# Output projections that accumulate in five PSUM banks in turn instead of two

## The chip, the cores and the metric

The kernel runs on one core of one Trainium2 chip. The metric is the device time of one execution in microseconds (us). Before the change it is 3158.45 us, the median of three runs that took 3152.99 to 3162.29 us.

## The reference

Four layers act in turn on x, 1024 tokens by 1024 features, all in float32. Every one of them ends in a projection back to 1024 features, and that last projection is what the change is about:

```python
# layer 1: dilated attention          return (o * jax.nn.silu(z)) @ w_out
# layer 2: state space (S5)           return (y * jax.nn.silu(z)) @ w_out
# both:                               x = x + rms_norm(h, post_norm)
# layers 3 and 4: hybrid layers (convolution, retention, neighbourhood attention)
y = jnp.concatenate([y_conv, y_ret, y_na], axis=-1) @ w_out
x_new = layer_norm(DEEPNORM_ALPHA * x + gate[:, None] * y, ln_g, ln_b)
```

The first hybrid layer (here: layer 0 of the hybrid part) also carries a context of 256 tokens through the same projection; the second (layer 1) does not.

## The kernel before

**Numbers in halves.** A float32 product is made of three products of two halves: every operand is split into a high part and a remainder (`aTh`/`aTl` for the activations, `wh`/`wl` or `wo` for the weights), and `mm3` (line 163) issues high·high, high·low and low·high for each of eight blocks k of 128 features. So one output tile of 128 tokens by 512 features is 24 matmuls of 128x128 by 128x512 that accumulate in one PSUM bank.

**PSUM.** The eight banks are dealt out by tag: `mm` has two (line 143, all projections), `T` two (transposes), `S` three (scores of the attentions, states of the retention), `O` one. A tile of a tag takes the bank of the tile that many places earlier under the same tag, and waits until the last reader of that one is done. An output tile's bank is read by VectorE (line 1166 after the first two layers, line 2074 in the hybrid layers), which multiplies by a gain or a gate; after the first two layers ScalarE also squares it (line 1165).

**The last projections.** `out_tile` (line 1102) makes one tile. `out_rms` (line 1144) calls it for eight blocks of 128 tokens and two halves of the features, 16 tiles, after dilated attention and after the state space layer; `out_ln` (line 2036) does so in the hybrid layers, 20 tiles in layer 0 (eight blocks and two of the context) and 16 in layer 1. Behind each block follow the norm and, but for the last layer, transposes of the result (line 219).

**What is late at the start of a hybrid layer's last projection.** The activations come in slabs of 256 tokens: each is fetched from DRAM by ScalarE's queue (lines 2013, 2014, into `ys`) and split by ScalarE and VectorE (lines 2017, 2018). Two output tiles come out of every block of 128 tokens, so a slab feeds four output tiles. The weight blocks 0 to 2 are split early into buffers of the attention that are free by then; blocks 3 to 5, and a slab that lies in the same pool, can start only when the neighbourhood attention has left its pool, after its last matmuls (`O`, lines 133 and 139, in the context 1944). The attention's end runs between the first output tiles on TensorE: transposes of the probabilities (lines 1861, 1870, 1932), products with the values, and a transpose for the weights of the sum (line 1903).

**Order.** The order of every engine's instructions is fixed when the kernel is built: a scheduler places them by its own estimates and by the waits that buffers and banks make. An engine then works strictly in that order.

Of the kernel before, what the change touches and what calls it, by code (L numbers as in the profile page):

```python
# [11 lines left out]
F32 = mybir.dt.float32  # L12
# [8 lines left out]
S = 1024  # L21
# [54 lines left out]
class Ker:  # L76
    def __init__(self, nc, tc, es, A):
        self.nc, self.tc, self.A = nc, tc, A
        self.cp = es.enter_context(tc.tile_pool(name="cp", bufs=1))
        self.big = es.enter_context(tc.tile_pool(name="big", bufs=1))  # L80
        self.ps = es.enter_context(tc.tile_pool(name="ps", bufs=1, space=PSUM))
        self.dr = es.enter_context(tc.tile_pool(name="dr", bufs=1, space=DRAM))
        self.wp = es.enter_context(tc.tile_pool(name="wp", bufs=1, reuse_waits="tile"))
        self.bg = deque()
        self.hot = deque()
        self.rate = 0.0
        self.acc = 0.0
        self.n = 0
        self.ident = self.cp.tile([128, 128], F32, name="ident")
        make_identity(nc, self.ident)  # L90
        self.mhalf = self.cp.tile([128, 1], F32, name="mhalf")
        nc.vector.memset(self.mhalf, -0.5)
        self.ones = self.cp.tile([128, 1], F32R, name="ones")
        nc.vector.memset(self.ones.bitcast(F32), 1.0)
        self.cact = self.cp.tile([128, 2, 8], F32, name="cact")
        self.hp = self.cp.tile([128, 1], F32, name="hp")
        nc.vector.memset(self.hp, math.pi / 2)
        self.fh = self.cp.tile([128, 32], F32R, name="fh")
        self.rest = self.cp.tile([128, 32], F32, name="rest")
        self.aTh = self.big.tile([128, 8, 1024], F32R, name="aTh")  # L100
        self.aTl = self.big.tile([128, 8, 1024], F32R, name="aTl")

    def uid(self, s):
        self.n += 1
        return f"{s}_{self.n}"
# [995 lines left out]

    def out_tile(self, i, nh, ks, aT=None):

        ps = self.mm()
        aT = (self.aTh, self.aTl) if aT is None else aT
        tt, c = slice(i * 128, i * 128 + 128), slice(nh * 512, nh * 512 + 512)
        self.mm3(ps, [((aT[0][:, k, tt], aT[1][:, k, tt]), (self.wo[k][0][:, c], self.wo[k][1][:, c]))
                      for k in ks])
        return ps
# [1065 lines left out]
```

## Time and profile before

| | |
|---|---|
| median of three runs | 3158.45 us (3152.99 to 3162.29) |
| profiled execution | 3156.31 us, its span 3154.1 us |
| TensorE (PE) busy | 3060.2 us, 97% of the span |
| VectorE (DVE) busy | 1894.4 us, 60% |
| ScalarE (ACT) busy | 1189.4 us, 38% |
| GpSimd (POOL) busy | 588.6 us, 19% |
| granted clock of TensorE, mean | 0.989 of full |

TensorE works nearly all the time. What it doesn't work, or works at half its clock, has to be looked for in short stretches; the table only says that such stretches are few.

### The profile page before, as it was taken

To read this page: it belongs to the slowest core of one execution; us is meant where nothing else is said; L and a number is where in the kernel's file an instruction comes from. 1 tells how busy PE (TensorE), PEld (TensorE's weight loads), DVE (VectorE), ACT (ScalarE), POOL (GpSimd) and SP (SyncE) were. 2 spreads that over 40 slices of the span, in tenths; PEclk is the share of its full clock that TensorE was granted. 3 is DMA by queue.
4 is the path that set the end of the run, shared out by engine and by line. 5 is a ranking of instruction groups with operands and counts; after the bars stand their busy time and mean duration, and the time that the engine had idled before them with its cause. 6 is when DMAs were issued, how large, how long until landed. Compare 5 with 4: busy or idle time off the path is not lost. (4 is left out here: it accounts for less than half of the span.)

```text
span 3154.1 us, 47830 instructions
## 1 busy us (share of the span) xinstructions
PE 3060.2 (97%) x18100; PEld 2539.2 (81%) x18100; DVE 1894.4 (60%) x4099; ACT 1189.4 (38%) x2492; POOL 588.6 (19%) x762
## 2 busy tenths in 40 slices
PE   8999999999999999999999999999998999999998
PEld 6777878778887878787878888788887888888877
DVE  4676676677766647665654634455566754455564
ACT  4222555455555554322431112244352212234351
POOL 0365120221211201110003122310001112220001
PEclk9999999999999999999999999999999999999999
DMA  5455232332333235565342211122125321121132
GB/s 200 152 187 175 69 102 83 88 103 83 96 95 97 76 102 181 184 181 156 121 144 90 81 43 57 48 82 60 48 72 170 104 73 56 54 81 52 51 119 94
DMA packets 332603, 324.11 MB, mean 103 GB/s; under 512 B 30073, under 2 KB 273492, under 8 KB 332372
## 3 DMA queue, kind: packets, MB, share of 16 engines
q1 hardware_dynamic: 324020, 312.79, 32.4%
q10 hardware_dynamic: 8352, 8.26, 0.8%
q8 instruction: 143, 2.34, 0.3%
q14 instruction: 88, 0.72, 0.1%
HBM read 248.29 MB, written 72.69 MB: 102 GB/s over the span
## 5 line engine op out<-in xcount | busy, mean ns | idle before, releaser
L172 PE MATMUL mm<-aTh,wh 128*128 128x512 f32 x2304 | 916.9, 398 | 12.9 <-DVE qk L427 2.9
L172 PE MATMUL mm<-aTl,wh 128*128 128x512 f32 x2304 | 913.0, 396 | 0.4 <-DVE aTl L225 0.2
L172 PE MATMUL mm<-aTh,wl 128*128 128x512 f32 x2304 | 912.8, 396 | 0.5 <-DVE wl L159 0.4
L172 PEld LDWEIGHTS mm<-aTh,wh 128*128 128x128 f32 x2304 | 436.6, 190 | 103.5 <-issue 4.6
L172 PEld LDWEIGHTS mm<-aTh,wl 128*128 128x128 f32 x2304 | 435.9, 189 | 87.0 <-DVE wl L159 1.4
L172 PEld LDWEIGHTS mm<-aTl,wh 128*128 128x128 f32 x2304 | 436.3, 189 | 84.5 <-issue 1.0
L159 DVE TENSOR_TENSOR wl<-wr,wh 128x1024 fp32r<-128x1024 f32 x156 | 197.6, 1267 | 221.9 <-ACT wh L158 220.6
L158 ACT ACTIVATE wh<-wr 128x1024 fp32r<-128x1024 f32 x156 | 164.9, 1057 | 325.3 <-PE mm L172 266.9
L172 PE MATMUL mm<-wo,aTh 128*128 128x512 f32 x768 | 247.3, 403 | 17.4 <-DVE ys L2074 9.0
L479 ACT ACTIVATE sb<-sb,st 128x128 f32<-128x128 f32 (+1 forms) x384 | 170.2, 445 | 240.0 <-DVE st L477 235.1
L1217 DVE SCALAR_TENSOR_TENSOR ma<-mw,cact,ma 128x256 f32<-128x256 f32 x336 | 184.3, 553 | 15.3 <-DMA mw<-in_w_mod 8.6
L172 PEld LDWEIGHTS mm<-wo,aTh 128*128 128x128 f32 x768 | 146.1, 193 | 51.3 <-DVE ys L2074 8.2
L477 DVE CUSTOM_DVE_ANT_0 sb<-S,bt 128x128 f32<-128x128 f32 (+1 forms) x384 | 125.5, 344 | 52.1 <-PE T L490 37.0
L172 PE MATMUL mm<-wo,aTl 128*128 128x512 f32 x384 | 153.0, 398 | 0.0
L431 POOL CAST qk<-kz 64x512 fp32r<-64x512 f32 x64 | 64.8, 1012 | 323.1 <-ACT kz L425 311.6
L1831 ACT ACTIVATE nsb<-nsb,nmn 128x640 f32<-128x640 f32 (+1 forms) x108 | 85.6, 793 | 101.8 <-DVE nmn L1828 97.7
L172 PE MATMUL mm<-vh,aTl 128*128 128x512 f32 x288 | 113.8, 395 | 0.0
L172 PE MATMUL mm<-vl,aTh 128*128 128x512 f32 x288 | 113.6, 394 | 0.0
L172 PE MATMUL mm<-vh,aTh 128*128 128x512 f32 x288 | 113.5, 394 | 0.0
L490 PE MATMUL T<-ident,sb 128*128 128x128 f32 x560 | 102.3, 285 | 9.9 <-ACT PT L493 6.1
L172 PE MATMUL mm<-cTh,wh 128*128 128x256 f32 x352 | 101.6, 289 | 0.6 <-DVE nk L1515 0.6
L172 PE MATMUL mm<-cTh,wl 128*128 128x256 f32 x352 | 100.3, 285 | 0.6 <-DVE wl L159 0.6
(449 smaller groups left out, 5624.3 us busy)
## 6 DMA issues: line engine op xcount, KB each, us to landing
wr<-in_attn_w_in SPq DMA_DIRECT2D x80, 512.0 KB
wr<-in_w_in SPq DMA_DIRECT2D x64, 512.0 KB
mw<-in_w_mod SPq DMA_DIRECT2D x48, 512.0 KB
vd<-vo SPq DMA_DIRECT2D x48, 256.0 KB
Wb<-wgd SPq DMA_DIRECT2D x96, 128.0 KB
x<-x SPq DMA_DIRECT2D x24, 512.0 KB
x<-in_x SPq DMA_DIRECT2D x16, 512.0 KB
V<-vd SPq DMA_DIRECT2D x32, 256.0 KB
```

What stands on the lines that cost most here:

```text
L158: nc.scalar.activation(h, raw, AF.Copy)
L159: nc.vector.tensor_tensor(l, raw, h.bitcast(F32), op=ALU.subtract)
L172: nc.tensor.matmul(out, s_, m_, start=first and i == 0, stop=last and i == len(todo) - 1)
L431: nc.gpsimd.tensor_copy(at(t[o], g, hf), at(h_[r], g, hf))
L477: nc.vector.tensor_tensor_reduce(out=sb[:, :N], in0=sp[:, a * 256:a * 256 + N], in1=b, scale=1.0, scalar=3e38, op0=ALU.add, op1=ALU.min, a ...
L479: nc.scalar.activation(sb[:, :N], sb[:, :N], AF.Exp, bias=mc, scale=-1.0, accum_out=st[:, 1, g, a, n:n + 1])
L490: nc.tensor.transpose(t[:, c:c + 128], Ps[a][:, b * 128:b * 128 + 128], self.ident)
L1217: V.scalar_tensor_tensor(a, L[h][:, k], c, a, op0=ALU.mult, op1=ALU.add)
L1831: ACT.activation(sb[:, :n], sb[:, :n], AF.Exp, bias=mc, scale=-1.0, accum_out=den)
```

## The change

`out_tile` counts its calls. The first and third of every five still take an `mm` bank; the second, fourth and fifth take one of the three `S` banks. The count runs on over all four layers (16, 16, 20 and 16 calls).

```diff
+
+    outs = 0
...
     def out_tile(self, i, nh, ks, aT=None):
 
-        ps = self.mm()
+        self.outs += 1
+        ps = (self.ps.tile([128, 512], F32, tag="S", name=self.uid("S"), bufs=3) if self.outs % 5 in (2, 4, 0)
+              else self.mm())
         aT = (self.aTh, self.aTl) if aT is None else aT
```

No instruction is added or taken away, but the scheduler moves some. Lines behind line 101 stand two or more lines later in the changed kernel.

TensorE in hybrid layer 0, where the last projection begins, before. Tiles `mm_22219` and `mm_22245` are the first two output tiles, `wo` the weights, `T_21879` and `O_21894` the attention of the context:

```order
L172 MATMUL mm_22219<-wo_22050,aTh 128x512
L172 MATMUL mm_22219<-wo_22049,aTl 128x512
L1932 MATMUL T_21879<-ident,nsb_21875 128x128 x2
L1944 MATMUL O_21894<-nPT_21869,nVc_21238 64x128
L172 MATMUL mm_22245<-wo_22037,aTh 128x512
L172 MATMUL mm_22245<-wo_22038,aTh 128x512
L172 MATMUL mm_22245<-wo_22037,aTl 128x512
```

The same place now; `S_22245` and `S_22276` are the second and third output tiles:

```order
L174 MATMUL S_22245<-wo_22050,aTh 128x512
L174 MATMUL S_22245<-wo_22049,aTl 128x512
L174 MATMUL S_22276<-wo_22037,aTh 128x512
L174 MATMUL S_22276<-wo_22038,aTh 128x512
L1936 MATMUL T_21879<-ident,nsb_21875 128x128 x2
L1948 MATMUL O_21894<-nPT_21869,nVc_21238 64x128
L174 MATMUL S_22276<-wo_22037,aTl 128x512
```

The transposes of the context's attention stood behind 9 matmuls of output tiles and stand behind 20. Up to the last group of `O` there are 9 more before, and 16 now: four tiles, not two, have gone through weight blocks 0 to 2 by then.

ScalarE's queue at that place before; `ys_22058` is the slab that feeds output tiles 5 to 8, `ys_22194` the slab of the context, `ys_22180` another slab of tokens:

```order
L2017 ACTIVATE aTh<-ys_22180 128x6x256
L158 ACTIVATE wo_22061<-wr_22059 128x1024
L158 ACTIVATE wo_22066<-wr_22064 128x1024
L158 ACTIVATE wo_22071<-wr_22069 128x1024
L2013 DMA ys_22058<-yd_16221 128x256
L2014 DMA ys_22058<-yd_16221 128x6x256
L2013 DMA ys_22194<-yd_16221 128x256
```

And now:

```order
L2021 ACTIVATE aTh<-ys_22180 128x6x256
L2017 DMA ys_22194<-yd_16221 128x256
L160 ACTIVATE wo_22061<-wr_22059 128x1024
L160 ACTIVATE wo_22066<-wr_22064 128x1024
L160 ACTIVATE wo_22071<-wr_22069 128x1024
L2017 DMA ys_22058<-yd_16221 128x256
L2018 DMA ys_22058<-yd_16221 128x6x256
```

The context's fetch, which waits for VectorE's split of `ys_22180`, has moved ahead of the splits of weight blocks 3 to 5 (`wo_22061`, `wo_22066`, `wo_22071`) and of the fetch of the next slab.

TensorE in hybrid layer 1 just before the last unit of the attention, before (`T_27844` holds its transposes):

```order
L172 MATMUL mm_28111<-wo_27968,aTh 128x512
L172 MATMUL mm_28137<-wo_27968,aTh 128x512
L172 MATMUL mm_28111<-wo_27969,aTh 128x512
L172 MATMUL mm_28111<-wo_27968,aTl 128x512
L172 MATMUL mm_28111<-wo_27974,aTh 128x512
L172 MATMUL mm_28137<-wo_27969,aTh 128x512
L172 MATMUL mm_28137<-wo_27968,aTl 128x512
L172 MATMUL mm_28137<-wo_27974,aTh 128x512
L172 MATMUL mm_28111<-wo_27975,aTh 128x512
L172 MATMUL mm_28137<-wo_27975,aTh 128x512
L1861 MATMUL T_27844<-ident,nsb_27804 128x128 x4
```

The end of the same stretch now; `mm_28194` and `S_28168` are the fourth and third output tiles:

```order
L174 MATMUL S_28168<-wo_27968,aTh 128x512
L174 MATMUL S_28168<-wo_27969,aTh 128x512
L174 MATMUL S_28168<-wo_27968,aTl 128x512
L174 MATMUL S_28168<-wo_27974,aTh 128x512
L174 MATMUL mm_28111<-wo_27975,aTh 128x512
L174 MATMUL S_28137<-wo_27975,aTh 128x512
L174 MATMUL S_28168<-wo_27975,aTh 128x512
L174 MATMUL mm_28194<-wo_27975,aTh 128x512
L1865 MATMUL T_27844<-ident,nsb_27804 128x128 x4
```

Ten matmuls of output tiles stood in this stretch, and 20 do now; between `T_27844` and the last `O` group there were eight, and there are 16, with the transposes of line 1903 ahead of that group too. In the state space layer four output tiles are begun side by side as well; in dilated attention's last projection little moves.

## Rows read from the trace of the kernel before

**Rows 1.** The page: busy time by engine (share of the span) and instructions.

```profile
PE 3060.2 (97%) x18100; PEld 2539.2 (81%) x18100; DVE 1894.4 (60%) x4099; ACT 1189.4 (38%) x2492; POOL 588.6 (19%) x762
```

**Rows 2.** Stretches, the last projections: us; PE, PEld, DVE, ACT, POOL busy; clock; DMA.

```profile
1211.00:1301.00 90.00, 90.00 (x422) 74.98 (x421) 77.06 (x115) 41.08 (x83) 16.99 (x35) 1.00 0.43 148
1641.00:1738.00 97.00, 94.30 (x444) 78.19 (x443) 45.29 (x49) 24.36 (x51) 26.01 (x34) 1.00 0.30 104
2361.00:2500.00 139.00, 130.25 (x592) 105.59 (x591) 99.36 (x145) 34.37 (x52) 17.71 (x30) 0.95 0.44 143
3040.00:3145.00 105.00, 97.55 (x440) 76.97 (x438) 58.82 (x91) 25.32 (x37) 15.03 (x22) 0.97 0.40 134
```

**Rows 3.** Chain of waits, hybrid layer 0: start us, us, what (with its count).

```profile
2368.51 12.51 DMA ys<-yd
...
2384.97 14.12 PE mm L172 x48
...
2485.21 11.04 PE mm L172 x48
```

**Rows 4.** Timeline of PE, layer 0: start us, us, instruction, [idle before, releaser].

```profile
2361.67 0.63 PE L172 MATMUL mm<-wo,aTh 128*128 128x512 f32 x2
...
2366.91 1.09 PE L1944 MATMUL O<-nPT,nVc 128*64 128x128 f32 x14
2370.11 0.87 PE L172 MATMUL mm<-wo,aTh 128*128 128x512 f32 x2 [2.11 <-ACT wo L158]
2372.09 0.80 PE L172 MATMUL mm<-wo,aTh 128*128 128x512 f32 x1 [1.12 <-DVE wo L159]
...
2377.62 0.39 PE L172 MATMUL mm<-wo,aTl 128*128 128x512 f32 x1
...
2384.97 1.22 PE L172 MATMUL mm<-wo,aTh 128*128 128x512 f32 x2 [3.74 <-DVE ys L2074]
...
2391.08 0.40 PE L172 MATMUL mm<-wo,aTl 128*128 128x512 f32 x1
```

**Rows 5.** Timeline of DVE at the same place.

```profile
2370.82 3.49 DVE L159 TENSOR_TENSOR wo<-wr,wo 128x1024 fp32r<-128x1024 f32 x3
...
2382.56 1.76 DVE L2018 TENSOR_TENSOR aTl<-ys,aTh 128x1536 fp32r<-128x1536 f32 x1 [7.35 <-ACT aTh L2017]
2384.23 0.68 DVE L2074 TENSOR_TENSOR ys<-mm,gate 128x512 f32<-128x512 f32 x1
```

**Rows 6.** Chain of waits, hybrid layer 1.

```profile
3051.33 9.32 DMA ys<-yd
...
3064.60 80.19 PE mm L172 x336
```

**Rows 7.** Timeline of PE, hybrid layer 1.

```profile
3040.24 0.73 PE L172 MATMUL mm<-wo,aTh 128*128 128x512 f32 x2
3041.63 0.50 PE L172 MATMUL mm<-wo,aTh 128*128 128x512 f32 x1 [0.66 <-DVE wo L159]
...
3044.37 0.66 PE L1861 MATMUL T<-ident,nsb 128*128 128x128 f32 x4 [0.52 <-ACT nPT L1864]
...
3050.18 0.61 PE L139 MATMUL O<-nPT,nVc 128*64 128x128 f32 x8
...
3064.60 1.22 PE L172 MATMUL mm<-wo,aTh 128*128 128x512 f32 x2 [3.58 <-DVE ys L2074]
...
3070.54 0.39 PE L172 MATMUL mm<-wo,aTl 128*128 128x512 f32 x1
```

**Rows 8.** Timeline of DVE, layer 1: the last read of an `S` bank of scores.

```profile
3041.49 0.42 DVE L1824 CUSTOM_DVE_ANT_0 nsb<-S,zero 128x256 f32<-128x256 f32 x1
```

**Rows 9.** Timeline of PE, the state space layer's last projection.

```profile
1654.85 0.72 PE L172 MATMUL mm<-wo,aTh 128*128 128x512 f32 x2 [2.54 <-DVE hs L1166]
```

**Rows 10.** Stretches: tiles side by side in layer 1; after the wait in layer 0.

```profile
3054.60:3060.60 6.00, 6.00 (x26) 4.62 (x25) 4.42 (x5) 1.50 (x3) 0.00 (x0) 1.00 0.88 326
...
2384.90:2390.50 5.60, 5.53 (x13) 4.42 (x14) 4.83 (x9) 2.90 (x4) 1.76 (x3) 0.50 0.76 242
```

## The prediction

> **What bounds the kernel now.** The page comes first: TensorE's matmuls fill 97% of the span, and of the other engines none is busy over 60% [rows 1]. So time can be won only where TensorE stands still or runs slowly, and the change touches it only in the last projections. The second view is therefore the busy time by stretches over those four stages [rows 2]. The reader is to see that the four differ: dilated attention's 90.00 us have no idle time at all, the state space layer's 97.00 us have 2.70, hybrid layer 0 has 139.00 - 130.25 = 8.75, layer 1 has 105.00 - 97.55 = 7.45. The clock column says the rest: 1.00 in the first two, 0.95 and 0.97 in the hybrid ones.
>
> The third view is TensorE's timeline at the beginnings of these stages, where nearly all of it lies. In layer 0 [rows 4] it waits 2.11 and 1.12 us for weight blocks that are being split, and then 3.74 us for a bank: tiles 1 and 2 are done, both `mm` banks are full, and VectorE empties the first only at 2384.23, because ahead of it in its order stands the split of a slab that ScalarE's copy, and so a DMA, keeps it waiting for [rows 5]. The chain of waits tells the same: the DMA of 12.51 us that was issued when the attention had ended, then the 48 matmuls of tiles 3 and 4 in 14.12 us, although 48 take 11.04 us where nothing disturbs [rows 3]. This last difference is the clock. From 2372.09 to 2377.62 there are 13 matmuls at 425 ns each, from 2384.97 to 2391.08 there are 14 at 436 [rows 4], against 11.04/48 = 230 ns; the granted clock there is 0.50, the lower level of 1.2 GHz instead of 2.4 [rows 10]. Both times TensorE had just stood still. Layer 1 has the same picture: 3.58 us for a bank, then 14 matmuls in 5.94 us [rows 7], behind a DMA of 9.32 us [rows 6].
>
> **The change part by part.** No instruction comes or goes; the 68 tiles keep their 24 matmuls. What changes is how many tiles may be open at once: five instead of two. A slab feeds four tiles, so up to four can now use the weight blocks as they come, and a fifth can begin on the next slab.
>
> Dilated attention's projection has no idle time to win [rows 2]: 0.
>
> State space layer: one wait of 2.54 us for a bank, with no loss of clock behind it [rows 9]. Its third tile has its own bank now, and its tokens are split before that point, as those of the first block were. -2.5; bounds 0 and -2.7, the stretch's whole idle time.
>
> Hybrid layer 0. Lost at the opening are 2.11 + 1.12 + 3.74 = 6.97 us of standing still and (425 - 230) x 13 + (436 - 230) x 14 = 5.4 us by the clock, together 12.4. Tiles 3 and 4 bring 48 matmuls, 11.0 us, that need nothing but slab 1 of the tokens and the same weights, so they fill these places. Part of it stays. The attention of the context stands behind 11 more matmuls and then 7 more (20 against 9, 16 against 9, as the order shows), which is 18 x 0.23 = 4.1 us; its last group, which began at 2366.91 and took 1.09 [rows 4], ends at about 2372.1. VectorE splits a weight block in 3.49/3 = 1.16 us [rows 5]; behind the attention's last product, which it has to read first (some 0.4 us), that gives the third block's remainder at 2373.7, while TensorE has used up the four high parts by 2373.0: 0.7 us of waiting. For the first transposes, which hang on a norm that starts no earlier than before while TensorE is ahead, I allow 1.3 us (an estimate; 0 to 4). So 2.0 us stay: -10.4. The next slab's fetch goes out with the attention's end, 4 us later, and lands 12.51 us behind [rows 3], at about 2385.0; with 1.5 us on ScalarE and 1.7 on VectorE [rows 5] it is ready at 2388.2. Tiles 1 to 4 end at about 2387.4, and tile 5 needs that slab only from its third weight block on. That is just in time, and the thinnest place of this sum. The context's fetch, moved ahead in ScalarE's queue, waits for a VectorE split that before ended where the weights' begins, at 2370.82 [rows 5]; the attention ends later than that, so it costs nothing, unless that split slips. Bounds: 0 and -12.4.
>
> Hybrid layer 1. Lost are 7.45 us of idle time [rows 2] and (5.94/14 - 0.23) x 14 = 2.7 us by the clock [rows 7]: 10.2. Three things stay or come. Tile 2 now takes the `S` bank of the last unit's scores, which VectorE reads until 3041.9 [rows 8]; TensorE gets there at 3040.5, so it waits about 1.5 us, where before it waited 0.66 for weights [rows 7]. The attention's last unit stands behind 10 and then 8 more matmuls. Its transposes had an idle time of 0.52 ahead of them [rows 7]; they come at 3044.37 - 0.52 + 10 x 0.23 = 3046.2, 1.8 us later, and its last products, which began at 3050.18, another 8 x 0.23 = 1.8 us on top, 3.6 in all. Weight block 3 can be split only then: 1.2 us of waiting for its high part and 0.3 for its remainder, taken from the splits' 1.16 us on VectorE [rows 5]. Together 3.0 us stay: -7.2. The next slab lands 9.32 us behind the attention's end [rows 6] and has 4 us to spare, since tiles 1 to 4, that ended at 3064.60 + 80.19 - 288 x 0.23 = 3078.5 [rows 6], end near 3071. Bounds: 0 and -10.2.
>
> Sum: -2.5 - 10.4 - 7.2 = -20.1 against the profiled execution's 3156.31 (span 3154.1), so 3136.2. That execution lies 2.14 below the median of 3158.45; of the median's kind the forecast is **3138.4 us**. Outside these stages TensorE is the bound as well [rows 1], so the gain is carried to the end.
>
> A rule that speaks against the change is about the clock. Here tiles that took turns in two banks ran at clock 1.00, 26 matmuls in 6.00 us [rows 10]; the low level came only behind idle times. By this row the openings run at 230 ns a matmul, as summed. The Trainium skill (TensorE: Matmul & The Clock Gate, A second HAM failure mode: psum-queue depth-cycling) says that a stream that cycles through PSUM banks can make TensorE idle so often between groups that its clock swings between the two levels. By that rule the sum would not be -20.1 but the third rival's.
>
> **The rivals.** *First: the attention's end slips further.* If the matmuls put ahead of it hold it back by 3 us more in each hybrid layer, tile 5 of layer 0 waits 3 us and falls to the low level for 14 matmuls (2.9), and layer 1 waits 3 more for weights: -20.1 + 8.9 = -11.2, 3147. For it: that slab has no margin. Against it: in both layers an idle time ahead of the attention's steps was there to be used [rows 7].
>
> *Second: the gain is given back.* VectorE is busy 99.36 of layer 0's 139.00 us [rows 2], and with 10 us less it would be at 77%; it starts on the evictions no earlier, and must catch up. If it doesn't, the five banks fill and TensorE waits again, later in the stage: layer 0's term goes and some of layer 1's, and less than 9.5 us is left, 3149 to 3158. That is also the outcome if the `S` banks are held longer than I read, so that the tiles stand in line as before. Against it: 139 us have room for 99.
>
> *Third: slower.* The 4 x 24 matmuls of the first four tiles in both hybrid layers, 192 in all, take turns in four banks. If that itself brings the low level, each costs 436 - 230 = 206 ns more [rows 3, 4]: +39.6, so 3178. It decides the sign from 98 such matmuls on (20.1/0.206). For it, only that the low level did come in these openings; against it the stretch at 1.00 [rows 10]. It is what the Trainium skill's rule above would make of this kernel.
>
> **How the numbers follow.** My forecast, 3132 to 3146, has a chance of 0.59; the first rival 0.21; the second 0.14; the third, with whatever else makes it slower, 0.06. A measurement of this kernel can tell about 0.3%, 9.5 us, from no change. Faster by more: 0.59 + 0.21 = 0.80; the same: 0.14; slower: 0.06. The range starts where all 25.3 us (2.7 + 12.4 + 10.2) come back, 3133, less the 5 us by which the runs before lay below or above their median: 3128. It ends at 3152, with the first rival and a few us behind it, and leaves out the larger part of the second and the third.
>
> **What would show it.** In the profile after: waits for VectorE's `ys` (line 2074 before) and `hs` gone from TensorE's timeline; the openings at clock 1.00; the attention's last products 3 to 4 us later against the first output tile; waits for `wo` of 1 to 2 us still there; both hybrid stretches 7 to 10 us shorter, the state space one 2.5, the first none. The prediction is wrong if TensorE waits for a slab at tile 5, if waits for banks come back in the middle of layer 0's stage, or if the stage is shorter and the next one longer.

## The result, and the profile after

The changed kernel takes 3136.41 us, the median of six runs (3133.25 to 3146.02), against 3157.22 us (six runs, 3152.99 to 3166.10) before it: a ratio of 0.993, 95% interval 0.9919 to 0.9942. The forecast was 3138.4 us. The profiled execution took 3136.05 us with a span of 3134.0, which is 20.1 less than the 3154.1 before and, to the tenth, the sum that was predicted. The stages show that this agreement is partly luck: from the first stage that gained to the end 25.7 us were won (25.1 in the projections), and 5.6 were lost ahead of it, where the change touches nothing but dilated attention's projection, which takes 90.00 us as before. Of these 5.6 us 4.5 were lost before that projection's first output matmul (at 1211.7 before, at 1216.2 now), so ahead of anything that the change moves.

Line numbers from here on are those of the changed kernel, two or four higher than before. The page's busy line, to be read beside [rows 1]:

```profile
PE 3052.7 (97%) x18100; PEld 2535.0 (81%) x18100; DVE 1891.1 (60%) x4099; ACT 1189.9 (38%) x2492; POOL 587.9 (19%) x762
```

The four last projections, in stretches that begin and end at the same points of the program as those of [rows 2]; columns as there:

```profile
1215.45:1305.45 90.00, 90.00 (x423) 74.98 (x421) 77.74 (x115) 40.80 (x83) 15.70 (x35) 1.00 0.42 148
1646.60:1740.70 94.10, 94.10 (x446) 78.50 (x445) 45.31 (x49) 24.55 (x51) 27.11 (x34) 1.00 0.31 107
2363.33:2489.24 125.91, 124.64 (x591) 101.56 (x591) 98.66 (x145) 34.40 (x52) 16.71 (x30) 1.00 0.49 158
3029.02:3124.90 95.88, 93.78 (x440) 75.41 (x438) 58.22 (x91) 25.32 (x37) 13.95 (x22) 1.00 0.43 147
```

Against 90.00, 97.00, 139.00 and 105.00 us before, the stretches are 0, 2.9, 13.1 and 9.1 us shorter, 25.1 together. The two hybrid ones can be split by their own columns. Layer 0's idle time falls from 8.75 to 1.27 us and TensorE's busy time from 130.25 to 124.64; layer 1's from 7.45 to 2.10 and from 97.55 to 93.78. The work is the same. Of the fall in busy time, 5.6 and 3.8 us, the low clock had cost 5.4 and 2.7, by the starts of the matmuls behind the waits. In layer 1 no more of it can be the clock, which was at 1.00 up to the wait for a bank:

```profile
3040.00:3060.00 20.00, 16.36 (x101) 11.57 (x100) 14.49 (x20) 11.96 (x19) 0.61 (x1) 1.00 0.74 248
```

The rest belongs to the edges of the waits. A matmul lasts 0.39 us here and the next one starts 0.23 behind its start; but the last one ahead of a wait overlaps with no other, and the first behind it takes 0.50. So a wait costs some 0.27 us more than its idle time (an estimate: 0.39 - 0.23 + 0.50 - 0.39), and layer 1 has four listed waits fewer. The clock is at 1.00 in all four stretches now.

TensorE in layer 0, the timeline that answers to [rows 4]: the first output tile, the transposes and the last products of the context's attention, every wait of the opening, the end of tiles 1 to 4, and the one later wait.

```profile
2364.00 0.63 PE L174 MATMUL mm<-wo,aTh 128*128 128x512 f32 x2
...
2368.59 0.38 PE L1936 MATMUL T<-ident,nsb 128*128 128x128 f32 x2
...
2373.37 1.09 PE L1948 MATMUL O<-nPT,nVc 128*64 128x128 f32 x14
2374.77 0.51 PE L174 MATMUL mm<-wo,aTh 128*128 128x512 f32 x1 [0.32 <-ACT wo L160]
...
2375.59 1.02 PE L174 MATMUL mm<-wo,aTh 128*128 128x512 f32 x2
...
2389.27 0.39 PE L174 MATMUL mm<-wh,aTl 128*128 128x512 f32 x1
2389.50 0.40 PE L174 MATMUL S<-wo,aTl 128*128 128x512 f32 x1
...
2411.53 1.06 PE L221 MATMUL T<-ident,ys 128*128 128x128 f32 x8 [0.72 <-DVE ys L2093]
```

The attention's last products begin 9.37 us after the first output tile, against 5.24 before: 4.13 later, as worked out (4.1). Of 2.11, 1.12 and 3.74 us of waiting 0.32 are left, and 0.12 inside the row at 2375.59: its two matmuls take 1.02 us, 0.39 and 0.51 without a wait between them. Four tiles are done 25.5 us after the start (25.7 predicted). The wait for VectorE's `ys` of 0.72 us is one for the norm.

VectorE at the same place, beside [rows 5]: the split of the late slab, and the first eviction behind it.

```profile
2386.91 1.76 DVE L2022 TENSOR_TENSOR aTl<-ys,aTh 128x1536 fp32r<-128x1536 f32 x1 [5.95 <-ACT aTh L2021]
2388.58 0.68 DVE L2078 TENSOR_TENSOR ys<-mm,gate 128x512 f32<-128x512 f32 x1
```

The order is that of before: the eviction still stands behind the split, and the split still waits for ScalarE and the DMA. The first bank is not emptied before 2388.58, 24.6 us into the stage. But TensorE has had work until then.

TensorE in layer 1, beside [rows 7]: the first and second output tile, all waits, the transposes and the last products of the attention.

```profile
3029.26 0.50 PE L174 MATMUL mm<-wo,aTh 128*128 128x512 f32 x1
3029.59 0.40 PE L174 MATMUL S<-wo,aTh 128*128 128x512 f32 x1
...
3030.83 0.50 PE L174 MATMUL mm<-wo,aTh 128*128 128x512 f32 x1 [0.61 <-DVE wo L161]
...
3034.85 0.60 PE L1865 MATMUL T<-ident,nsb 128*128 128x128 f32 x4
...
3042.33 0.61 PE L141 MATMUL O<-nPT,nVc 128*64 128x128 f32 x8
3044.10 0.50 PE L174 MATMUL mm<-wo,aTh 128*128 128x512 f32 x1 [1.16 <-ACT wo L160]
```

And VectorE there, where scores were to hold tile 2's bank [rows 8]:

```profile
3027.36 0.61 DVE L1832 CUSTOM_DVE_ANT_0 nsb<-S,tab,nmn 128x384 f32<-128x384 f32 x1
...
3030.69 0.42 DVE L1828 CUSTOM_DVE_ANT_0 nsb<-S,zero 128x256 f32<-128x256 f32 x1
...
3033.31 0.61 DVE L1832 CUSTOM_DVE_ANT_0 nsb<-S,tab,nmn 128x384 f32<-128x384 f32 x1
```

Tile 2 begins at 3029.59 without a wait for its bank, while VectorE reads two banks of scores only from 3030.69 and 3033.31 on. So it has the third one, whose reader began at 3027.36.

### The profile page after: what moved, and what is told of

Read it like the earlier page. It is cut to its first block, busy times and chain, and to the rows that moved or that the text cites. A ratio compares the mean times of both kernels' runs of the same rounds, so it can differ in the third digit from the quotient of the medians.

```text
span 3134.0 us, 47825 instructions
## 1 busy us (share of the span) xinstructions
PE 3052.7 (97%) x18100; PEld 2535.0 (81%) x18100; DVE 1891.1 (60%) x4099; ACT 1189.9 (38%) x2492; POOL 587.9 (19%) x762
## 4 chain that ended last, share of the span: by engine, by line
PE 55%; DVE 3%; DMA 2%; issue 1%; ACT 1%; POOL 0%; SPq 0%; ACTq 0%; POOLq 0%; DVEq 0%
PE mm L174 38%; PE S L174 6%; PE S L1852 2%; PE T L1865 1%; PE O L141 1%; PE T L1560 1%; DMA ys<-yd 1%; PE T L221 1%; PE T L141 1%; PE S L1700 1%; PE S L954 1%; PE S L1627 1%; PE S L1685 0%; PE O L135 0%; DMA cs<-csd 0%
## 5 line engine op out<-in xcount | busy, mean ns | idle before, releaser
L174 PEld LDWEIGHTS mm<-aTh,wh 128*128 128x128 f32 x2304 | 436.3, 189 | 104.7 <-issue 4.3
L479 DVE CUSTOM_DVE_ANT_0 sb<-S,bt 128x128 f32<-128x128 f32 (+1 forms) x384 | 125.9, 345 | 51.4 <-PE T L492 37.2
L174 PE MATMUL S<-wo,aTh 128*128 128x512 f32 x444 | 140.0, 393 | 0.0
L174 PE MATMUL mm<-wo,aTh 128*128 128x512 f32 x324 | 104.1, 394 | 2.3 <-ACT wo L160 1.5
L174 PE MATMUL mm<-cTl,wh 128*128 128x256 f32 x352 | 100.4, 285 | 0.0
```

What stands on the lines that cost most here:

```text
L174: nc.tensor.matmul(out, s_, m_, start=first and i == 0, stop=last and i == len(todo) - 1)
L479: nc.vector.tensor_tensor_reduce(out=sb[:, :N], in0=sp[:, a * 256:a * 256 + N], in1=b, scale=1.0, scalar=3e38, op0=ALU.add, op1=ALU.min, a ...
```

## The experiments

Eleven runs were made, each beside the kernel before. The table gives for each profile, from TensorE's timeline and the span: when the state space layer's last projection begins, from its first output matmul to the last one that uses `wo`, start to start, the same for layer 0, from layer 1's first output matmul to the end of the span, and the whole from the state space projection on.

| kernel | median, us | before, us | ratio, 95% interval | begins | state space | layer 0 | layer 1, end | from there on |
|---|---|---|---|---|---|---|---|---|
| before | 3157.22 | | | 1641.3 | 93.7 | 132.8 | 113.9 | 1512.8 |
| after | 3136.41 | 3157.22 | 0.993, 0.9919 to 0.9942 | 1646.9 | 90.9 | 119.7 | 104.7 | 1487.1 |
| rms_only | 3155.62 | 3158.51 | 0.9994, 0.9982 to 1.0007 | 1643.8 | 90.9 | 132.7 | 114.2 | 1509.6 |
| l0_only | 3143.28 | 3158.51 | 0.995, 0.9935 to 0.9965 | 1642.3 | 95.3 | 123.1 | 114.9 | 1505.6 |
| l0_again | 3142.44 | 3157.13 | 0.9958, 0.9942 to 0.9974 | 1641.2 | 93.7 | 120.4 | 112.6 | 1499.0 |
| l1_only | 3149.95 | 3158.51 | 0.9972, 0.9959 to 0.9985 | 1646.5 | 93.7 | 132.9 | 105.1 | 1504.0 |
| four | 3129.18 | 3158.51 | 0.9906, 0.9893 to 0.9919 | 1640.0 | 90.9 | 119.3 | 105.1 | 1487.2 |
| five_again | 3131.94 | 3158.93 | 0.992, 0.9905 to 0.9936 | 1642.6 | 90.9 | 119.3 | 104.7 | 1487.0 |
| four_again | 3136.00 | 3158.93 | 0.993, 0.9916 to 0.9943 | 1643.0 | 90.9 | 119.9 | 104.7 | 1487.6 |
| three | 3138.56 | 3158.93 | 0.994, 0.9925 to 0.9954 | 1641.6 | 90.9 | 125.5 | 105.2 | 1493.9 |
| first5 | 3130.63 | 3158.93 | 0.9915, 0.99 to 0.9929 | 1637.7 | 90.9 | 121.0 | 104.6 | 1489.0 |
| two_pool | 3151.47 | 3159.28 | 0.998, 0.9968 to 0.9993 | 1635.8 | 95.3 | 133.5 | 108.7 | 1510.3 |
| five_pool | 3137.21 | 3159.28 | 0.9929, 0.9916 to 0.9943 | 1649.6 | 90.9 | 122.8 | 105.1 | 1491.2 |

### One stage at a time: rms_only, l0_only, l1_only

```diff
-        ps = (... if self.outs % 5 in (2, 4, 0)
+        ps = (... if self.outs % 5 in (2, 4, 0) and self.outs <= 32          # rms_only
+        ps = (... if self.outs % 5 in (2, 4, 0) and 32 < self.outs <= 52     # l0_only, l0_again
+        ps = (... if self.outs % 5 in (2, 4, 0) and self.outs > 52           # l1_only
```

> The S banks take turns only in the last projections of dilated attention and the state space layer; both hybrid layers keep two banks. Theory A (the three terms are real, and the 5.6 us by which the changed kernel reached the state space layer's last projection later are chance): 2.8 us faster than before, ratio 0.999, its TensorE wait for hs (line 1166 before) gone, the hybrid stretches as in the kernel before, with their waits for ys. Theory B (the change itself makes the work ahead of that projection 5.6 us longer): 2 to 3 us slower, ratio 1.001, with the state space layer's last projection beginning at about 1646.9 as in the changed kernel's profile, against 1641.3 before.

> The S banks take turns only in hybrid layer 0's last projection. Theory A (the terms are separate and add up): 13.1 us faster than before, ratio 0.9958: from its first output tile to the first transpose behind its last one 121.3 us as in the changed kernel, against 134.4; the state space layer keeps its wait for hs of 2.5 us and layer 1 its wait for ys of 3.6. My forecast's own term was 10.4. Theory C (the gain is given back further on): the stage is 13 us shorter and the following one longer, less than 8 us in all.

> The S banks take turns only in hybrid layer 1's last projection, at the program's end. Theory A: 9.1 us faster than before, ratio 0.9971: 104.7 us from its first output tile to the end of the span against 113.9. My forecast's own term was 7.2, with 1.5 us of waiting for the S bank of the last scores, which the changed kernel's profile did not show. Theory D (that wait did not show because a tile of another phase took the bank by chance): the wait comes here, and 7.5 us are won.

By the medians 2.9, 15.2 and 8.6 us were won; the intervals hold A's 2.8, 13.1 and 9.1, and that of rms_only holds no gain too, so there the wait for `hs`, gone from its profile, is the evidence. But for l0_only's profile, each stage that has its five banks takes what it takes in the changed kernel within 0.7 us, and the others stay as before, so the terms add up and nothing is given back in the next stage (C falls). In layer 1 alone tile 2 waits for no bank either (D falls). The beginning of the state space projection is at 1643.8 in rms_only; in l1_only, where everything up to there is two-bank code, it is at 1646.5, as late as in the changed kernel.

l0_only's profile fits badly: its state space projection, unchanged code, took 95.3 us, layer 0's 123.1. That execution was the kernel's slowest. The same kernel once more:

> Five banks only in layer 0's last projection, once more, since the first profile of this kernel was its slowest execution (3149.97 against a median of 3143.28). Theory A: 12 to 16 us faster than before; layer 0's projection at 119 to 120 us as in the four profiles with four or five banks everywhere, and layer 1's 113.9 to the end. Theory L (the term of layer 0 depends on the state space layer's banks): again 123 us, with the wait of 2 us for ys (line 2093) ahead of the second group of transposes.

Now it is 120.4, and 13.8 us less from the state space projection on; L's 123 falls. From there on rms_only, l0_again and l1_only win 3.2, 13.8 and 8.8 us, 25.8 together, against 25.7 for all at once. The wait for the norm ahead of the second group of transposes was 1.99 us in the one execution and 1.46 in the other; with five or four banks everywhere it was 0.72, 0.35, 0.32 and 0.98. Why it is longer where layer 0 alone has the banks stays open.

What made the state space projection longer is the clock. The same 11.5 us behind the same wait of 2.54 us, from the windows of the kernel before:

```profile
1654.77:1666.27 11.50, 11.42 (x52) 9.45 (x53) 3.92 (x5) 0.83 (x4) 3.33 (x4) 1.00 0.39 131
```

and of l0_only:

```profile
1655.76:1667.26 11.50, 11.42 (x43) 9.26 (x44) 3.92 (x5) 0.71 (x3) 3.32 (x4) 0.85 0.38 134
```

TensorE is busy equally long, but makes 43 matmuls instead of 52, at a granted clock of 0.85, so part of the stretch is at 1.2 GHz. The wait cost 2.5 us in one execution and 1.6 more in another.

### How many banks: five_again, four, four_again, three

```diff
-        ps = (... if self.outs % 5 in (2, 4, 0)
+        ps = (... if self.outs % 2 == 0        # four, four_again
+        ps = (... if self.outs % 3 == 1        # three
```

The names say how many tiles, in their order, find a bank that is free. `S` tiles still go round all three `S` banks: in layer 0 the fifth tile has to wait for the first one's bank in four, and the fourth in three, but the sixth, or the fifth in three, can already begin in a bank of its own.

> Four banks instead of five: every second tile takes an S bank, the others the two of projections, so a fifth tile waits for the first. Theory A (a slab feeds four tiles, and nothing can be multiplied behind them until the next slab has come, at about 24.6 us after the stage's start in layer 0): within 1 us of five banks, that is about 21 to 25 us faster than before, ratio 0.9925 to 0.9935. Theory E (every bank more is worth something, since evictions come late): 3 us or more behind five banks, with waits for ys (the gate's product) on TensorE at the fifth tile.

> The changed kernel once more, beside four banks on the same chip. Theory A: what stands ahead of the state space layer's last projection varies by chance from run to run (1640.0 to 1646.9 us in the profiles so far, although every engine's order is the same there), and the rest is settled: 90.9 us for that projection, 119.7 for layer 0's and 104.8 from layer 1's to the end, each within 0.5. Then 22 to 28 us faster than before, 25.0 by the terms. Theory B (the change makes that first part longer): about 20, with that part again above 1645.

> Four banks once more. Theory A: its lead of 8 us on five banks was chance in the first part, since its stages took the same time; now within 3 us of five banks. Theory G (something in four banks is really better): again 6 us or more ahead of five.

The first time four banks were 29.3 us faster than before, the second time 22.9; five banks were 20.8 and 27.0. Their stages took the same time in all four profiles, 1487.0 to 1487.6 us from the state space projection on. So which of the two is ahead changes from one time to the other, a bank of its own for the fifth tile is worth nothing that shows, and theories E and G fall. Five profiles (before, l0_only, l0_again, l1_only, two_pool) have the same order on every engine up to the state space layer's last projection, and begin it between 1635.8 and 1646.5 us, on average at 1641.4. The eight with S banks in dilated attention's projection begin it between 1637.7 and 1649.6, on average at 1643.1. That is this kernel's noise, and theory B's 5 us fall with it: five_again begins at 1642.6 and gains 27.0. A cost of one or two us there is not excluded.

> Three banks: every third tile takes an S bank, and a fourth tile waits for the first. Theory A (the banks bridge the time until the late slab has been split, because the evictions stand behind that split in VectorE's order): the state space layer's projection is at 90.9 us (its wait was 2.5 us, one tile is 5.5); in layer 0 the work for three tiles and the attention runs out after about 20 us, the slab's split is over at about 24, so a wait for ys of 3 to 4 us comes back, with the low clock behind it: 125 to 127 us; layer 1 has 0 to 2 us of wait: 105 to 107. In all 15 to 19 us faster than before. Theory E (each bank more is worth the same): a third of five banks' gain, 8 us. Theory H (three are enough): 23 us or more.

Layer 0 took 125.5 us, the whole from the state space projection on was 18.9 us shorter than before, and both are where A put them (by the medians it is 20.4). The place was a different one, by TensorE's timeline of three:

```profile
2375.24 2.07 PE L174 MATMUL S<-wo,aTh 128*128 128x512 f32 x4 [3.26 <-ACT aTh L2021]
2377.11 0.63 PE L174 MATMUL mm<-wo,aTh 128*128 128x512 f32 x1
```

and its clock just behind:

```profile
2375.24:2381.09 5.85, 5.85 (x15) 4.61 (x15) 0.41 (x1) 1.03 (x1) 0.00 (x0) 0.53 1.12 346
```

The wait is as long as expected, but not for an eviction. The fourth tile has no bank, so the scheduler put the first products of later tiles, on the next slab, ahead of some thirty matmuls of the first three tiles (from 2377.11 on), and TensorE waits for the slab itself. The low clock follows, 15 matmuls in 5.85 us. So the loss comes with three banks, but by the order; that the work of three tiles would run out is not shown by this run.

### Where in the stage: first5

```diff
+        ps = (... if self.outs % 5 in (2, 4, 0) and any(a < self.outs <= a + 5 for a in (0, 16, 32, 52))
```

> Only the first five tiles of each of the four projections take turns in five banks, all later ones have the two banks of before. Theory A (the gain lies at the openings): the three stages within 1 us of five banks, 24 to 26 us faster than before by the terms; perhaps the wait of 1.7 us for ys that the kernel before had 40 us into layer 0 comes back. Theory C2 (the later tiles need the banks too): waits for ys in the middle of layer 0's stage, 3 us or more lost.

From the state space projection on it takes 1489.0 us, 1.9 more than five banks throughout; layer 0, at 121.0, is a little outside A's 1 us. In layer 0 one wait that the kernel before had as 1.66 us is back, in TensorE's timeline:

```profile
2394.39 0.74 PE L174 MATMUL mm<-wo,aTh 128*128 128x512 f32 x2 [1.96 <-DVE ys L2078]
```

So the openings hold nearly all of it (C2 falls), and this one wait is the rest.

### Why two banks stalled: two_pool and five_pool

In both, GpSimd makes the remainders (line 2022) of the second slab and of the context's; two_pool has two banks, five_pool five.

```diff
...
-                put(th, tl, 0, c, Y[i][:, 0])
-                put(th, tl, slice(2, 8), c, Y[i][:, 2:8])
+                put(th, tl, 0, c, Y[i][:, 0], nc.gpsimd if i in (1, 4) else V)
+                put(th, tl, slice(2, 8), c, Y[i][:, 2:8], nc.gpsimd if i in (1, 4) else V)
...
```

> Two banks as before the change; GpSimd instead of VectorE makes the remainders of the late slab (the second one of tokens) and of the context's slab, so that on VectorE the evictions of the first two tiles no longer stand behind a split that waits for a DMA. Theory A (two banks stall because of that order): the first waits for ys fall from 3.7 and 3.6 us to about 1 (one product of 0.68 us and its signals), and some of the low clock behind them goes; layer 0's projection 127 to 129 us against 132.8, layer 1's to the end 109 to 111 against 113.9; 7 to 11 us faster than before, less than half of what five banks give, since the waits for weights and the attention's end stay open. Theory J (the evictions wait for something else): both stages as before, with waits for ys of 3.5 us or more.

VectorE's timeline in layer 0 of two_pool:

```profile
2375.65 0.69 DVE L2078 TENSOR_TENSOR ys<-mm,gate 128x512 f32<-128x512 f32 x1 [5.24 <-PE mm L174]
...
2377.49 0.69 DVE L2078 TENSOR_TENSOR ys<-mm,gate 128x512 f32<-128x512 f32 x1 [0.41 <-PE mm L174]
...
2383.42 1.28 DVE L2092 SCALAR_TENSOR_TENSOR ys<-ys,ls,nsc 128x1024 f32<-128x1024 f32 x1 [4.51 <-POOL ls L2087]
```

GpSimd's and TensorE's there:

```profile
2378.70 3.61 POOL L2022 TENSOR_TENSOR aTl<-ys,aTh 128x1536 fp32r<-128x1536 f32 x1 [6.67 <-ACT aTh L2021]
```

```profile
2391.21 1.94 PE L221 MATMUL T<-ident,ys 128*128 128x128 f32 x8 [2.72 <-DVE ys L2093]
...
2396.33 1.19 PE L174 MATMUL mm<-wo,aTh 128*128 128x512 f32 x2 [3.18 <-DVE ys L2078]
```

The evictions now wait only for TensorE, and the first wait for a bank is gone: 3.74 us in layer 0 to none, 3.58 in layer 1 to 0.33. That shows A's reason. In layer 1 it pays 5.1 us with two banks. In layer 0 all of it is given back: the norm's small step on GpSimd stands behind the remainder of 3.61 us, VectorE waits 4.51 us for it and then needs 3.2 us more than elsewhere for a step of its own (below), and TensorE waits 2.72 and 3.18. So A's 127 to 129 was wrong, and layer 0 shows what the second rival would have looked like. That the medians differ by 7.8 us, inside A's 7 to 11, is luck: from the state space projection on 2.5 were won.

> Five banks, and the same remainders on GpSimd, which needs 1.3 to 1.5 us for 128x512 (rows of the kernel before), so some 4 us for the 128x1536 of the late slab, where VectorE needs 1.76. Theory A (tile 5 of layer 0 gets its slab just in time, and that is the thin place): the slab is ready some 2 to 3 us later, TensorE waits about 2 us at tile 5 and may fall to the low clock behind it: layer 0's projection 121 to 124 us against 119.5 of five banks; layer 1, with 4 us to spare, as with five banks, 104.7 to the end. Theory K (VectorE's load holds the stage): layer 0's projection gets shorter, 118.5 or less.

GpSimd's and TensorE's timelines in layer 0 of five_pool:

```profile
2389.36 3.55 POOL L2022 TENSOR_TENSOR aTl<-ys,aTh 128x1536 fp32r<-128x1536 f32 x1 [5.64 <-ACT aTh L2021]
```

```profile
2393.19 0.62 PE L174 MATMUL S<-wo,aTh 128*128 128x512 f32 x2
...
2401.66 1.06 PE L221 MATMUL T<-ident,ys 128*128 128x128 f32 x8 [2.33 <-DVE ys L2093]
```

The size was right, 122.8 us, and the reason wrong. Tile 5 asks for that slab from 2393.19 on, its third weight block, and the remainder was there at 2392.91: no wait. What cost 2.33 us, and a clock of 0.77 in the 7.34 us behind, is again the norm. It is late because two of VectorE's steps last far longer than elsewhere. VectorE's timeline of five_pool, and GpSimd's remainder of the context:

```profile
2389.51 3.94 DVE L2081 SCALAR_TENSOR_TENSOR ys<-ys 128x512 f32<-128x512 f32 x1
...
2397.00 4.52 DVE L2093 SCALAR_TENSOR_TENSOR ys<-ys,rs,nsh 128x1024 f32<-128x1024 f32 x1 [0.45 <-POOL rs L202]
```

```profile
2396.92 3.51 POOL L2022 TENSOR_TENSOR cTl<-ys,cTh 128x1536 fp32r<-128x1536 f32 x1
```

In the changed kernel these steps take 0.69 and 1.28 us. Here the first begins while GpSimd makes the slab's remainder and the second while it makes the context's, and each ends 0.5 to 1.1 us behind GpSimd's step. In two_pool the second one takes 4.52 us as well, from 2386.55 on, beside a remainder that began at 2386.47; TensorE's 2.72 us there are less than what this adds. Evictions, which read a bank, took 0.69 us each beside such a remainder (layer 1 of five_pool, 3061.35 and 3062.03). What makes the difference was not tried.

In the changed kernel the slab is ready at 2388.6 and asked for from 2390.43 on, so the thin place has 1.8 us.

## Why the prediction was right, and where only its sum was

**State space layer.** -2.5 predicted, -2.9 measured, the wait for `hs` gone. Right, but for the edges of that wait, which the sum and its bound of 2.7 left out; and priced at one execution: where the low clock follows the wait it is worth 1.6 more.

**Layer 0.** -10.4 predicted, -13.1 measured. The mechanism was right and the term too small. "So 2.0 us stay" is the step that failed: 0.44 us stayed at the opening. The waits for weights came out at 0.32 + 0.12 instead of 0.7, and the 1.3 allowed for the first transposes was not needed. Besides, the sum listed 6.97 us of standing still out of 8.75 [rows 2] and left the rest uncounted, in it the 1.66 us that first5 brings back; with five banks 0.72 of waiting for the norm stands in that part of the stage. 12.4 + 1.66 - 0.44 - 0.72 = 12.9; the 0.2 left are of the size of the edges. So the gain lies beyond the bound of 12.4, and the sign "both hybrid stretches 7 to 10 us shorter" was missed here.

**Layer 1.** -7.2 predicted, -9.1 measured. "Tile 2 now takes the `S` bank of the last unit's scores" failed: the turn of the banks gave it another one, and the 1.5 us never came, here or in l1_only; the early wait for weights, which it was to replace, stayed, with 0.61 us (0.66 before). The waits for weight block 3, 1.2 + 0.3 predicted, were 1.16 and 0.07. The clock had cost the 2.7 us reckoned; the other 1.0 of the busy time that went fits the edges of four waits (4 x 0.27), a term that the sum put at nothing. The attention's last products came 3.1 us later against the first output tile (3.6 predicted).

**The sum.** The stages gave 25.1 us, the forecast said 20.1, and the profiled execution showed 20.1 because it reached the state space projection 5.6 us later than the one before, where profiles of the same code lie up to 10.7 apart. The second measurement gave 27.0. A forecast of the effect, not of a median, should have said 25.

**The rivals.** The attention's end slipped no further than reckoned (the idle time ahead of its steps, claimed for both layers, is there in layer 1 alone; in layer 0 no wait is listed ahead of them), and the slab arrived in time; its fetch landed 10.1 us behind its issue, not 12.5. Banks did not fill later in the stage, which at 125.9 us has VectorE at 78% (98.66 busy). The third rival, low clock through turns in four banks, did not come: the granted clock is 1.00 in all four stretches. The Trainium skill's rule (TensorE: Matmul & The Clock Gate, A second HAM failure mode: psum-queue depth-cycling) names idling between groups as what makes the clock swing. The trace agrees in so far as the low level was seen behind idle times only in these projections, and turns without them ran at 2.4 GHz.

## What to carry to other kernels

A PSUM bank is free when its reader's queue comes to it, not when the product is done: if evictions stand behind a step that waits for a late transfer, count how many tiles of work TensorE needs until that transfer has landed, and give them that many banks (here 24.6 us, less 3.5 of other work, which is 25.5 less four tiles at 5.5, makes 3.8 tiles: four). That four tiles are enough is measured; that three are too few by this count is not, and a kernel that has only four banks in all was not run. Moving the blocking step to another engine frees the banks as well, but whatever small step stands behind it there is late in its place, and beside GpSimd's remainders here steps of VectorE lasted 3.2 us longer. And when an effect is near the noise, add it up over the stages that the change touches: their times agreed within 0.6 us over four profiles of four and five banks, whose first parts differed by 6.9.

## What was not expected of the hardware

The same idle time does not always bring the low clock: behind a wait of 2.5 us in the same code the clock stayed at 1.00 in before, l1_only and l0_again, and was 0.85 over the next 11.5 us in l0_only and two_pool. What decides it stays open. The first 1640 us vary by 10.7 us over five profiles with the same order on every engine. About half of it is waiting and half slower matmuls: up to the state space layer's last projection TensorE idles 54.3 us and is busy 1581.5 in the shortest (two_pool), and 59.9 and 1586.6 in the longest (l1_only), over the same matmuls. What makes them vary stays open; the start of dilated attention's last projection already lay between 1205.9 and 1217.3. Nor was it expected that steps of VectorE would last longer while GpSimd works: 3.94 us instead of 0.69, 4.52 instead of 1.28 (five_pool).
